# Hybrid decoder trunk on one core: loads and casts two chunks ahead, activation parts side by side, transposes behind products

## The chip, the cores and the metric

The kernel runs on one core of a Trainium2 chip. The metric is device time in microseconds of one launch, the median of several runs. The engines are named as in the profile: PE is TensorE (PEld its weight loads), DVE is VectorE, ACT is ScalarE, POOL is GpSimd, SP is the SyncE queue that issues all DMAs here.

## What is computed

Two layers over 256 tokens of 1024 channels, in float32. Cut to what matters here:

```python
hn = rms_norm(x, norm1_g)
proj = hn @ w_in                      # 1024 x 8216, 15 pieces
o_gla = gla_mixer(g_q, g_k, g_v, log_sigmoid(g_a @ up + b) / 16)     # decay per channel
mq, mk = (apply_rope(rms_norm(heads(a), g)) for a in (m_q, m_k))
y_moba = moba_mixer(mq, mk, m_v)      # softmax attention, 8 heads of 64
h_ml = mlstm_mixer(conv(l_q), conv(l_k), l_v, log_i, log_f)
gates = sigmoid(br_gate + gate_b)     # three branches of 1024
mixed = gates[0] * (y_gla @ w_gla) + gates[1] * (y_moba @ w_moba) + gates[2] * (y_mlstm @ w_mlstm)
x = x + mixed @ w_out
x = x + square(relu(rms_norm(x, norm2_g) @ w_ff1)) @ w_ff2
```

## The kernel before, in words

**Chunks.** All large weights lie in memory as chunks of 128 x 2048 floats (1 MB), 74 per layer, and the list ORDER (lines 152 to 155) fixes in which order they are used, both layers in a row. `prepare` (158) loads a chunk into one of three raw buffers with a DMA on SP and calls `split` (143): ACT rounds the chunk to the fast fp32r type as `hi`, DVE computes the rest `lo = raw - hi`, both in two halves of 128 x 1024, into one of three buffers each. `chunk` (171) hands out a chunk and first prepares all up to AHEAD (26) chunks behind it. The activations are kept in the same two parts: class `Norm` (189) writes `h` on ACT and `l` on DVE, channels on partitions. Each product of two numbers is then three matmuls: hi x h, lo x h, hi x l.

**Kinds of products.** `tok` (288) takes two chunks (a = 0, 1) and makes 256 tokens x 512 channels: per chunk 24 matmuls of 512 columns into two PSUM banks, one per token half. `chan_pair` (241) takes one chunk and makes 256 channels x 256 tokens, weights stationary: 48 matmuls of 256 columns into one bank. It makes gq, gk, lq (664 to 678) and the 16 chunks of `ff1` (775) of each layer. PSUM has eight banks: four in the pool pmm for these products, four in pmx for transposes and small products.

**A layer.** First the small weights ("s"), then mk (chunks 10, 11), the first gate (20, 21), mq (8, 9), the second gate (22, 23), mv, gv, gq, gk, and so on. `rope` (346) evicts mk or mq scaled by the norm factor (`scaled`, 301), squares and sums it, and rotates it with tables; of the two token halves DVE takes one and POOL the other (358). The decays of the GLA branch are the small products z (397 to 406), then logarithms, running sums and the exponentials eb and en (435 to 452; en is multiplied on POOL). The three mixers moba, gla and mlstm are generators, advanced a step at a time between the projections (646 to 725), the rest of mlstm behind the last gate. Then for each half of the channels three branch products br (728 to 740), each multiplied by its gate on DVE, the sum taken on DVE or, for the second branch, on POOL; then the transposes mt of the result (743 to 750), the output projection wo (753 to 769), the second norm, and the feed-forward part: ff1 of one chunk alternating with ff2 of another (775 to 827).

**What sets the order.** The framework's scheduler puts each engine's instructions into one fixed order at build time, by a priority that follows the program text and by when its cost model expects the operands. `tc.high_priority()` moves a block up; `after(i, j)` (60) puts instruction i behind j on their engine without a wait. DMAs keep the order of issue on SP, and an issue waits there until its buffer is free.

The initial loads are in lines 99 to 105, `late_loads` (129) follows the first mk chunk. The head of the layer loop reads:

```python
sh, sl_ = chunk(l, "s")
if l == 0:
    for k in range(4, 8):
        norm.parts(k, xTs[1][:, k - 4])
...
bmk = []
tok("mk", 10, 0, bmk)
```

Of the kernel before, what the change touches and what calls it, by code (L numbers as in the profile page):

```python
# [10 lines left out]
F32R = mybir.dt.float32r  # L11
# [3 lines left out]
OP = mybir.AluOpType  # L15
# [10 lines left out]
AHEAD = 1  # L26
# [17 lines left out]
def kernel(ctx: ExitStack, tc: tile.TileContext, xT, xtok, gbias, wbig, wsml, aup, cst, prm, out):  # L44
# [48 lines left out]
    nc.scalar.preload_act_table_set("exp_and_others")  # L93
# [6 lines left out]
    nc.sync.dma_start(xTs[0][:, 0:2], xT[:, 0:2, :])  # L100
    nc.sync.dma_start(raws[0][:, :512], wsml[0][:, :512])
    nc.sync.dma_start(xTs[0][:, 2:4], xT[:, 2:4, :])
    nc.sync.dma_start(raws[0][:, 512:], wsml[0][:, 512:])
    for p in range(2):
        nc.sync.dma_start(xTs[1][:, 2 * p:2 * p + 2], xT[:, 4 + 2 * p:6 + 2 * p, :])

    ident = cs[:, C_ID:C_ID + P]
# [21 lines left out]
    def late_loads():  # L129
# [13 lines left out]
    def split(tag, raw, n):  # L143
        hi = wspl.tile([P, CHW], F32R, tag="hi", name=f"hi{tag}")
        lo = wspl.tile([P, CHW], F32R, tag="lo", name=f"lo{tag}")
        for c in range(0, n, n // 2):
            sl = slice(c, c + n // 2)
            nc.scalar.copy(hi[:, sl], raw[:, sl])  # L148
            nc.vector.tensor_sub(lo[:, sl], raw[:, sl], hi[:, sl])  # L149
        return hi, lo  # L150
# [90 lines left out]
    def chan_pair(name, w, rh, rl, ks=range(KT), bank=None):  # L241
# [33 lines left out]
    for k in range(4):  # L275
        norm.parts(k, xTs[0][:, k])

    for l in range(DEPTH):
# [22 lines left out]
        def scaled(name, bs):  # L301
            o = slab(name, shape=(P, 2, 512))
            for t in range(2):
                nc.scalar.activation(o[:, t], bs[t].t, AF.Copy, scale=r[:, t:t + 1])
            return o
# [3 lines left out]
        if l == 0:  # L309
            for k in range(4, 8):  # L310
                norm.parts(k, xTs[1][:, k - 4])
        sh, sl_ = (a[:, :D].rearrange("p (k c) -> p k c", c=P) for a in (sh, sl_))
        bsm = Bank(pmm, f"sm{l}", [P, 512])
# [7 lines left out]
        if l == 0:  # L321
            late_loads()
            for t in range(2):
                for n in range(2):
                    norm.squares(t, n)
# [16 lines left out]
        if l + 1 < DEPTH:  # L342
            nc.sync.dma_start(raws[l + 1], wsml[l + 1])


        def rope(w, nm, bs):
            u = scaled(nm + "u", bs)
# [9 lines left out]
            for t in range(2):  # L357
                eng = nc.vector if t == 0 else nc.gpsimd
# [3 lines left out]
                eng.tensor_mul(r3, u[:, t].rearrange("p (h d) -> p h d", d=64), c3)  # L362
# [31 lines left out]
        rok, rsk = rope(1, "mk", bmk)  # L394
# [3 lines left out]
        for p in range(2):  # L398
            b = Bank(pmx, f"z{l}{p}", [P, 2, T])
            for n in range(2):  # L400
                h = 2 * p + n
                b.mm(b.t[:, n], us[:, h * P:(h + 1) * P], gs, True, True)
            for n in range(2):
                h = 2 * p + n
                nc.vector.tensor_scalar(mz[:, h], b.t[:, n], ab[:, h:h + 1], 0.0, op0=OP.add, op1=OP.min)
                nc.scalar.activation(az[:, h], b.t[:, n], AF.Abs, bias=ab[:, h:h + 1])
# [9 lines left out]

        gates = []

        def gate(i):
            bias = half(f"gb{l}{i}")  # L420
            nc.sync.dma_start(bias, gbias[l, i])
            bs = []
            tok(f"bg{i}", 20 + 2 * i, 0, bs)
            tok(f"bg{i}", 20 + 2 * i, 1, bs)
            g = slab(f"gate{i}", shape=(P, 2, 512))
            gates.append(g)
            for t in range(2):
                nc.vector.scalar_tensor_tensor(g[:, t], bs[t].t, r[:, t:t + 1], bias, op0=OP.mult, op1=OP.add)  # L428
                nc.scalar.activation(g[:, t], g[:, t], AF.Tanh, scale=0.5)

        gate(0)
# [231 lines left out]
        for p in range(2):  # L663
            b = chan_pair(f"gq{l}{p}", chunk(l, 4 + p), xh, xl)
            nc.vector.tensor_mul(qd[:, 2 * p:2 * p + 2], b.t, eb[:, 2 * p:2 * p + 2])
            step(M)
        for p in range(2):
            b = chan_pair(f"gk{l}{p}", chunk(l, 6 + p), xh, xl)
            nc.vector.tensor_mul(ki[:, 2 * p:2 * p + 2], b.t, en[:, 2 * p:2 * p + 2])
            step(M)  # L670
# [6 lines left out]
        for p in range(2):  # L677
            b = chan_pair(f"lq{l}{p}", chunk(l, 14 + p), xh, xl)
            nc.vector.tensor_mul(lqk[:, 2 * p:2 * p + 2, 3:], b.t, rT2)
# [44 lines left out]
        for _ in range(12):  # L724
            step(L)
# [3 lines left out]
        for hf in range(2):  # L729
            for br, (yh_, yl_) in enumerate((yg, (ymh, yml), yl)):  # L730
                w = [a.rearrange("p (k c) -> p k c", c=512) for a in chunk(l, 32 + 2 * br + hf)]
                g = gates[2 * br + hf]
                for t in range(2):
                    ts = slice(t * P, (t + 1) * P)
                    b = Bank(pmm, f"br{l}{br}{hf}{t}", [P, 512])
                    for k in range(4):
                        rows_mm(b, w, k, slice(0, 512), yh_[:, k, ts], yl_[:, k, ts], k == 0, k == 3)
                    nc.vector.scalar_tensor_tensor(g[:, t], g[:, t], 1.0, b.t, op0=OP.add, op1=OP.mult)  # L738
                    if br:
                        (nc.gpsimd if br == 1 else nc.vector).tensor_add(g[:, t], g[:, t], gates[2 * br - 2 + hf][:, t])  # L740
# [10 lines left out]


        norm = Norm(f"b{l}", q[:, Q_G2:Q_G2 + 8])
        ob = [[Bank(pmm, f"wo{l}{t}{n}", [P, 512]) for n in range(2)] for t in range(2)]
        for a in range(2):
            for n in range(2):
                w = [z.rearrange("p (k c) -> p k c", c=512) for z in chunk(l, 38 + 2 * a + n)]
                for t in range(2):
                    ts = slice(t * P, (t + 1) * P)
                    b = ob[t][n]  # L760
# [14 lines left out]
        def ff1(p):  # L775
            b = chan_pair(f"f1{l}_{p}_", chunk(l, 42 + p), norm.h, norm.l)
# [3 lines left out]
            s = half(f"fs{p}", shape=(P, 2, T))  # L780
            nc.vector.tensor_scalar(s, b.t, 0.0, None, op0=OP.max)
            nc.scalar.activation(s, s, AF.Square)  # L782
# [161 lines left out]
```

## Time and profile before

| | us |
|---|---|
| median of 3 runs (lowest, highest) | 935.83 (934.37, 935.89) |
| profiled execution, whole time | 934.08 |
| profiled execution, span from first to last instruction | 932.3 |

The profile is of one execution. Busy times of PE are modelled at their ends, so a busy PE isn't PE at its peak; the start-to-start distance of products tells its rate. Time that an engine waits is put down to what came last. All sums are made against the profiled execution.

### The profile page before, as it was taken

The page shows a single profiled execution, that of the slowest core. Times are in us where ns is not written, and L with a number is a line of the kernel's source. Part 1 is how long each engine was busy: PE and PEld are TensorE (multiplying, and loading weights), DVE is VectorE, ACT ScalarE, POOL GpSimd, SP SyncE. Part 2 cuts the span into 40 slices and gives each one's busy share as a digit, 9 for nine tenths or more (in the row PEclk, how much of TensorE's full clock was granted, in tenths as well). Part 3 has the DMA queues.
Part 4 walks back from the last instruction along what each step waited for, and adds up shares of the span by engine and source line. Part 5 has one row for each costly group of instructions (what it writes and reads, how often), then busy time and mean ns, then how long its engine had stood idle before and what let it go on. Part 6 is the DMA issues. An engine that isn't in the chain of part 4 may idle for free.

```text
span 932.3 us, 12890 instructions
## 1 busy us (share of the span) xinstructions
PE 905.4 (97%) x5188; PEld 793.9 (85%) x5188; DVE 628.6 (67%) x992; ACT 454.0 (49%) x647; POOL 73.3 (8%) x90
## 2 busy tenths in 40 slices
PE   7799999999999999999999999999999999999998
PEld 5578999888789999999887789988877799999996
DVE  5996668568867655555669966766788675555553
ACT  5765544455336444444557564445543554444441
POOL 2552000000210000000002300000013000000000
PEclk9799999999999999999999999999999999999999
DMA  8646443545444555555543564344545555555541
GB/s 325 217 164 246 177 147 110 218 151 188 162 160 175 187 188 199 194 180 183 181 169 114 192 226 151 131 161 167 192 147 180 181 182 181 181 187 192 196 148 45
DMA packets 26203, 164.92 MB, mean 177 GB/s; under 512 B 3040, under 2 KB 3296, under 8 KB 7328
## 3 DMA queue, kind: packets, MB, share of 16 engines
q1 hardware_dynamic: 26144, 164.11, 49.6%
q8 instruction: 40, 0.66, 0.3%
q14 instruction: 19, 0.16, 0.1%
HBM read 163.05 MB, written 1.05 MB: 176 GB/s over the span
## 4 chain that ended last, share of the span: by engine, by line
PE 85%; DVE 11%; issue 1%; ACT 1%; DMA 1%; SPq 0%; POOL 0%; DVEq 0%; ACTq 0%
PE fa L75 19%; PE bg L75 10%; PE wo L75 5%; DVE lo L149 4%; PE br L75 3%; PE gk L75 2%; PE lq L75 2%; PE gq L75 2%; PE lv L75 2%; PE lo L75 2%; PE mv L75 2%; PE gv L75 2%; PE gg L75 2%; PE mk L75 2%; PE sc L75 1%
## 5 line engine op out<-in xcount | busy, mean ns | idle before, releaser
L148 ACT CAST hi<-raw 128x1024 fp32r<-128x1024 f32 x296 | 301.4, 1048 | 368.0 <-issue 97.8
L149 DVE TENSOR_TENSOR lo<-raw,hi 128x1024 fp32r<-128x1024 f32 x296 | 363.3, 1247 | 142.5 <-ACT hi L148 142.1
L75 PE MATMUL fa<-hi,fh 128*128 128x512 f32 x512 | 162.4, 390 | 0.0
L75 PEld LDWEIGHTS fa<-hi,fh 128*128 128x128 f32 x512 | 96.3, 188 | 19.6
L75 PE MATMUL fa<-lo,fh 128*128 128x512 f32 x256 | 100.0, 391 | 0.0
L75 PE MATMUL bg<-lo,xha 128*128 128x512 f32 x192 | 76.2, 397 | 4.8 <-DVE lo L149 4.8
L75 PE MATMUL bg<-hi,xha 128*128 128x512 f32 x192 | 76.8, 401 | 4.1 <-ACT hi L148 4.1
L75 PE MATMUL bg<-hi,xla 128*128 128x512 f32 x192 | 75.8, 395 | 0.0
L75 PEld LDWEIGHTS fa<-lo,fh 128*128 128x128 f32 x256 | 48.2, 188 | 8.9
L75 PEld LDWEIGHTS bg<-lo,xha 128*128 128x128 f32 x192 | 36.8, 191 | 13.5 <-DVE lo L149 6.4
L75 PEld LDWEIGHTS bg<-hi,xha 128*128 128x128 f32 x192 | 36.6, 191 | 11.5 <-ACT hi L148 4.3
L75 PEld LDWEIGHTS bg<-hi,xla 128*128 128x128 f32 x192 | 36.7, 191 | 7.7
L75 PE MATMUL wo<-hi,mh 128*128 128x512 f32 x64 | 25.7, 401 | 0.0
L75 PE MATMUL wo<-hi,ml 128*128 128x512 f32 x64 | 25.0, 391 | 0.0
L75 PE MATMUL wo<-lo,mh 128*128 128x512 f32 x64 | 24.9, 389 | 0.0
L428 DVE SCALAR_TENSOR_TENSOR gate<-bg,ny,gb 128x512 f32<-128x512 f32 x24 | 17.3, 748 | 7.7 <-PE bg L75 7.7
L784 DVE TENSOR_TENSOR fh<-fs,fh 128x512 fp32r<-128x512 f32 x32 | 21.9, 684 | 0.0
L782 ACT ACTIVATE fs<-fs 128x512 f32<-128x512 f32 x32 | 20.1, 627 | 0.0
L738 DVE SCALAR_TENSOR_TENSOR gate<-gate,br 128x512 f32<-128x512 f32 x24 | 16.3, 680 | 5.3 <-PE br L75 5.3
L783 ACT CAST fh<-fs 128x512 fp32r<-128x512 f32 x32 | 19.7, 617 | 0.0
L475 ACT ACTIVATE pe<-pe,mn 128x128 f32<-128x128 f32 (+1 forms) x32 | 14.3, 449 | 10.1 <-DVE mn L473 10.1
L75 PE MATMUL lq<-xha,hi 128*128 128x256 f32 x64 | 18.8, 294 | 0.0
(550 smaller groups left out, 2218.3 us busy)
## 6 DMA issues: line engine op xcount, KB each, us to landing
raw<-in_wbig_dram SPq DMA_DIRECT2D x147, 1024.0 KB, 4.8
gb<-in_gbias_dram SPq DMA_DIRECT2D x12, 256.0 KB, 3.2
xT<-in_xT_dram SPq DMA_DIRECT2D x4, 256.0 KB, 4.9
raw<-in_wbig_dram SPq DMA_DIRECT2D x4, 256.0 KB, 6.2
x<-in_xtok_dram SPq DMA_DIRECT2D x2, 512.0 KB, 8.8
out_dram<-x SPq DMA_DIRECT2D x4, 256.0 KB, 2.1
cs<-in_cst_dram SPq DMA_DIRECT2D x1, 768.0 KB, 10.2
raws<-in_wsml_dram SPq DMA_DIRECT2D x2, 256.0 KB, 4.1
```

The source lines that it names most:

```text
L75: self._chain(nc.tensor.matmul(o, lhsT=lhsT, rhs=rhs, start=start, stop=stop, skip_group_check=True))
L148: nc.scalar.copy(hi[:, sl], raw[:, sl])
L149: nc.vector.tensor_sub(lo[:, sl], raw[:, sl], hi[:, sl])
L428: nc.vector.scalar_tensor_tensor(g[:, t], bs[t].t, r[:, t:t + 1], bias, op0=OP.mult, op1=OP.add)
L475: nc.scalar.activation(pe[:, cols], pe[:, cols], AF.Exp, bias=mn[:, i], scale=-1.0, accum_out=sums[:, i])
L738: nc.vector.scalar_tensor_tensor(g[:, t], g[:, t], 1.0, b.t, op0=OP.add, op1=OP.mult)
L782: nc.scalar.activation(s, s, AF.Square)
L783: nc.scalar.copy(h[:, 0], s)
L784: nc.vector.tensor_sub(h[:, 1], s, h[:, 0])
```

## The change

Two chunks are prepared ahead instead of one. The first loads are issued by one loop in the same order; the input x is loaded ahead of the constants, and with it the first raw chunks; the parameters and small weights of layer 1 are loaded behind the first gate. The parts of the first norm and the split of the small weights are one high-priority block. `h` and `l` become one tile `hl` with the two parts side by side per channel block, and `chan_pair` multiplies the hi weights with both at once (512 columns) into two banks, one per 128 channels; ACT copies the half from `l` and DVE adds the other. The weights of these chunks are laid out for it. `rope` does both token halves on DVE, and the evictions of mk stand behind the casts of chunk 21. The z products (`decays`) go between the two chunks of the first gate. eb, en and dec come after the rotation of mq, en on DVE. The gate's first DVE step gets high priority. The last steps of mlstm go between the branch products, the transposes mt behind a later branch product and behind the first chunk of wo, and the second branch's sum to DVE.

```diff
-AHEAD = 1
+AHEAD = 2
...
+    def load_x():
         for t in range(2):
             nc.sync.dma_start(x[:, t], xtok[:, t])
+
+    def load_constants():
         nc.sync.dma_start(cs, cst)
...
-        for l in range(1, DEPTH):
-            nc.sync.dma_start(prm_t[l], prm[l])
...
+        behind[tag] = i, j
         return hi, lo
...
-            self.h = act.tile([P, KT, T], F32R, tag="xh", name=f"xh{tag}")
-            self.l = act.tile([P, KT, T], F32R, tag="xl", name=f"xl{tag}")
+            self.hl = act.tile([P, KT, 2, T], F32R, tag="xhl", name=f"xhl{tag}")
+            self.h, self.l = self.hl[:, :, 0], self.hl[:, :, 1]
...
-        wh, wl = (a.rearrange("p (k c) -> p k c", c=T) for a in w)
-        b = bank or Bank(pmm, name, [P, 2, T])
-        for k in ks:
-            for n in range(2):
-                c = slice(n * P, (n + 1) * P)
-                b.mm(b.t[:, n], wh[:, k, c], rh[:, k], k == 0 and n == 0, False)
-                b.mm(b.t[:, n], wh[:, k, c], rl[:, k], False, False)
-                b.mm(b.t[:, n], wl[:, k, c], rh[:, k], False, k == KT - 1)
-        return b
+        wh, wl = (a.rearrange("p (n k c) -> p n k c", n=2, c=P) for a in w)
+        for n in range(2):
+            b = Bank(pmm, f"{name}{n}", [P, 2, T])
+            for k in range(KT):
+                b.mm(b.t, wh[:, n, k], hl[:, k], k == 0, False)
+                b.mm(b.t[:, 0], wl[:, n, k], hl[:, k, 0], False, k == KT - 1)
+            nc.scalar.copy(os[n], b.t[:, 1])
+            nc.vector.tensor_add(os[n], os[n], b.t[:, 0])
...
-    for k in range(4):
-        norm.parts(k, xTs[0][:, k])
+
+    def first_parts(c):
+        for k in (range(2, 6) if c == 0 else range(6, 8)):
+            norm.parts(k, xTs[k // 4][:, k % 4])
+
+    with tc.high_priority():
+        for k in range(2):
+            norm.parts(k, xTs[0][:, k])
+        ready[0, "s"] = split("s0", raws[0], D, first_parts)
+    done[0] = 1
...
-        bsm = Bank(pmm, f"sm{l}", [P, 512])
+        bsm = Bank(pmx if l == 0 else pmm, f"sm{l}", [P, 512])
...
-                eng = nc.vector if t == 0 else nc.gpsimd
+                eng = nc.vector
...
-        rok, rsk = rope(1, "mk", bmk)
+        rok, rsk = rope(1, "mk", bmk, behind[f"{l}_21"])
...
+            tok(f"bg{i}", 20 + 2 * i, 0, bs)
+            between()
+            tok(f"bg{i}", 20 + 2 * i, 1, bs)
...
+        gate(0, decays)
+        if l + 1 < DEPTH:
+            nc.sync.dma_start(prm_t[l + 1], prm[l + 1])
+            nc.sync.dma_start(raws[l + 1], wsml[l + 1])
...
-        nc.gpsimd.tensor_mul(en, en, rT4)
-
-        tok("mq", 8, 1, bmq)
-        roq, rsq = rope(0, "mq", bmq)
+        nc.vector.tensor_mul(en, en, rT4)
...
-            b = chan_pair(f"gq{l}{p}", chunk(l, 4 + p), xh, xl)
-            nc.vector.tensor_mul(qd[:, 2 * p:2 * p + 2], b.t, eb[:, 2 * p:2 * p + 2])
+            chan_pair(f"gq{l}{p}", chunk(l, 4 + p), norm.hl, [qd[:, 2 * p + n] for n in range(2)])
+            nc.vector.tensor_mul(qd[:, 2 * p:2 * p + 2], qd[:, 2 * p:2 * p + 2], eb[:, 2 * p:2 * p + 2])
...
-        for _ in range(12):
-            step(L)
+        step(L)
...
+                    if br:
+                        nc.vector.tensor_add(g[:, t], g[:, t], gates[2 * br - 2 + hf][:, t])
+                if hf == 0:
+                    step(L)
+                elif br == 0:
+                    merged(0)
...
+                if a == 0 and n == 0:
+                    merged(1)
...
-            nc.vector.tensor_scalar(s, b.t, 0.0, None, op0=OP.max)
-            nc.scalar.activation(s, s, AF.Square)
+            nc.vector.scalar_tensor_tensor(s, s, 0.0, s, op0=OP.max, op1=OP.mult)
```

## Rows read from the trace of the kernel before

**Rows 1.** The page: busy time of each engine, and the last chain's shares by engine.

```profile
PE 905.4 (97%) x5188; PEld 793.9 (85%) x5188; DVE 628.6 (67%) x992; ACT 454.0 (49%) x647; POOL 73.3 (8%) x90
...
PE 85%; DVE 11%; issue 1%; ACT 1%; DMA 1%; SPq 0%; POOL 0%; DVEq 0%; ACTq 0%
```

**Rows 2.** The chain that ended last, in order of time: start us, us, what.

```profile
93.66 5.75 PE gq L75 x48
...
309.86 5.47 PE fa L75 x24
```

**Rows 3.** Waits of PE: line, waited for, us in total, times, longest.

```profile
PE sm L75 <- ACT his L148: 6.2, 1, 6.2
PE bg L75 <- DVE lo L149: 4.8, 3, 2.7
PE bg L75 <- ACT hi L148: 4.1, 1, 4.1
PE mt L78 <- DVE gate L740: 2.6, 4, 0.9
PE z L75 <- DVE gs L393: 2.1, 1, 2.1
PE mv L75 <- DVE lo L149: 1.1, 1, 1.1
PE yl0b L78 <- DVE ymls L627: 0.8, 1, 0.8
```

**Rows 4.** Windows: length, busy (count) of PE, PEld, DVE, ACT, POOL; clock, DMA, GB/s.

```profile
30.00:40.00 10.00, 8.09 (x25) 6.62 (x26) 10.00 (x21) 4.93 (x8) 3.38 (x3) 0.61 0.37 128
23.40:66.60 43.20, 34.89 (x141) 27.71 (x138) 41.82 (x58) 31.11 (x41) 21.90 (x20) 0.88 0.52 188
130.00:164.00 34.00, 34.00 (x225) 30.99 (x224) 29.24 (x68) 14.00 (x28) 0.11 (x1) 1.00 0.33 118
310.00:460.00 150.00, 150.00 (x956) 136.85 (x955) 83.68 (x83) 68.55 (x83) 0.00 (x0) 1.00 0.53 188
480.00:530.00 50.00, 46.30 (x205) 37.45 (x204) 46.40 (x66) 32.09 (x42) 14.55 (x12) 1.00 0.45 159
```

**Rows 5.** Timeline of PE in 23 to 48 us: start us, us, instruction [idle before].

```profile
27.96 1.22 PE L75 MATMUL bg<-hi,xha 128*128 128x512 f32 x2 [4.09 <-ACT hi L148]
31.91 0.80 PE L75 MATMUL bg<-lo,xha 128*128 128x512 f32 x1 [2.73 <-DVE lo L149]
```

**Rows 6.** Timeline of ACT, then DVE, in 9 to 72 us.

```profile
8.56 1.71 ACT L199 ACTIVATE xha<-xT,prm 128x256 fp32r<-128x256 f32 x4 [0.73 <-DMA xT<-in_xT_dram]
...
23.00 0.69 ACT L304 ACTIVATE mku<-mk,ny 128x512 f32<-128x512 f32 x1 [3.77 <-PE mk L75]
...
26.86 2.94 ACT L148 CAST hi<-raw 128x1024 fp32r<-128x1024 f32 x3
...
29.56 3.43 DVE L149 TENSOR_TENSOR lo<-raw,hi 128x1024 fp32r<-128x1024 f32 x2
```

**Rows 7.** Groups of DVE and POOL by line: busy us, mean ns | idle before.

```profile
L362 DVE TENSOR_TENSOR mkro<-mku,tabs 128x512 f32<-128x512 f32 x2 | 1.4, 686 | 2.0 <-ACT mku L304 2.0
L362 DVE TENSOR_TENSOR mqro<-mqu,tabs 128x512 f32<-128x512 f32 x2 | 5.8, 2898 | 0.0
L149 DVE TENSOR_TENSOR lo<-raw,hi 128x1024 fp32r<-128x1024 f32 x296 | 363.3, 1247 | 142.5 <-ACT hi L148 142.1
L740 POOL TENSOR_TENSOR gate<-gate,gate 128x512 f32<-128x512 f32 x8 | 14.0, 1765 | 36.9 <-DVE gate L738 36.9
L452 POOL TENSOR_TENSOR az<-az,rTa 128x1024 f32<-128x1024 f32 x2 | 6.5, 3254 | 24.4 <-ACT az L450 24.4
```

**Rows 8.** Groups of ACT and DVE that read 128x256 from PSUM.

```profile
L237 ACT COPY rTa<-nb2a 128x256 f32<-128x256 f32 x2 | 0.7, 354 | 0.0
L390 DVE TENSOR_TENSOR sm<-sm,rTa 128x256 f32<-128x256 f32 x2 | 0.8, 414 | 0.0
```

More of the change, by code (lines that the diff above doesn't have):

```diff
@@ L99 @@
     nc.sync.dma_start(prm_t[0][:, :Q_RG], prm[0][:, :Q_RG])
[L100 to L105, printed above, removed]
+    for p in range(4):
+        nc.sync.dma_start(xTs[p // 2][:, 2 * (p % 2):2 * (p % 2) + 2], xT[:, 2 * p:2 * p + 2, :])
+        if p < 2:
+            nc.sync.dma_start(raws[0][:, 512 * p:512 * p + 512], wsml[0][:, 512 * p:512 * p + 512])
+    nc.scalar.preload_act_table_set("exp_and_others")
     ident = cs[:, C_ID:C_ID + P]
@@ L141, with split @@
     nc.gpsimd.tensor_copy(ms[64:], rows[64:])
-    def split(tag, raw, n):
+    behind, evacuated = {}, {}
+    def split(tag, raw, n, between=lambda c: None):
         hi = wspl.tile([P, CHW], F32R, tag="hi", name=f"hi{tag}")
@@ L147, in split @@
             sl = slice(c, c + n // 2)
-            nc.scalar.copy(hi[:, sl], raw[:, sl])
-            nc.vector.tensor_sub(lo[:, sl], raw[:, sl], hi[:, sl])
+            i = nc.scalar.copy(hi[:, sl], raw[:, sl])
+            j = nc.vector.tensor_sub(lo[:, sl], raw[:, sl], hi[:, sl])
+            between(c)
+        behind[tag] = i, j
         return hi, lo
@@ L299, in tok, with scaled @@
                     bs[t].mm(bs[t].t, xl[:, kk, ts], wh[:, k], False, kk == 7)
-        def scaled(name, bs):
+        def scaled(name, bs, first=None):
             o = slab(name, shape=(P, 2, 512))
-            for t in range(2):
-                nc.scalar.activation(o[:, t], bs[t].t, AF.Copy, scale=r[:, t:t + 1])
+            with tc.high_priority():
+                for t in range(2):
+                    i = nc.scalar.activation(o[:, t], bs[t].t, AF.Copy, scale=r[:, t:t + 1])
+                    if first:
+                        after(i, first)
+            evacuated[name] = i
             return o
@@ L309 @@
         if l == 0:
-            for k in range(4, 8):
-                norm.parts(k, xTs[1][:, k - 4])
+            load_x()
         sh, sl_ = (a[:, :D].rearrange("p (k c) -> p k c", c=P) for a in (sh, sl_))
-        bsm = Bank(pmm, f"sm{l}", [P, 512])
+        bsm = Bank(pmx if l == 0 else pmm, f"sm{l}", [P, 512])
         for k in range(KT):
@@ L335 @@
         nc.gpsimd.tensor_sub(us[64:96], up[64:96], us[64:96])
+        hr = small("hr", [P, 2])
+        nc.gpsimd.tensor_scalar(hr, r, 0.5, None, op0=OP.mult)
         tabs = act.tile([P, 4, 2, 64], F32, tag="tabs", name=f"tabs{l}")
@@ L341, with rope @@
         tok("mk", 10, 1, bmk)
[L342 to L347, printed above, removed]
+        def rope(w, nm, bs, first=(None, None)):
+            u = scaled(nm + "u", bs, first[0])
             ss = small(nm + "ss", [P, 16])
@@ L361, in rope @@
                 c3 = tabs[:, 2 * w, t][:, None, :].to_broadcast([P, 8, 64])
-                eng.tensor_mul(r3, u[:, t].rearrange("p (h d) -> p h d", d=64), c3)
+                i = eng.tensor_mul(r3, u[:, t].rearrange("p (h d) -> p h d", d=64), c3)
+                if first[1]:
+                    after(i, first[1])
                 tmp = half(f"{nm}tmp{t}")
@@ L393, with gate, decays @@
         nc.vector.tensor_sub(gs[32:64], sm[32:64], gs[32:64])
-        rok, rsk = rope(1, "mk", bmk)
-        mz, az = slab("mz"), slab("az")
[L398 to L406, printed above, removed]
+        rok, rsk = rope(1, "mk", bmk, behind[f"{l}_21"])
+        gates = []
+        def gate(i, between=lambda: None):
+            bias = half(f"gb{l}{i}")
+            nc.sync.dma_start(bias, gbias[l, i])
+            bs = []
+            tok(f"bg{i}", 20 + 2 * i, 0, bs)
+            between()
+            tok(f"bg{i}", 20 + 2 * i, 1, bs)
+            g = slab(f"gate{i}", shape=(P, 2, 512))
+            gates.append(g)
+            with tc.high_priority():
+                for t in range(2):
+                    nc.vector.scalar_tensor_tensor(g[:, t], bs[t].t, r[:, t:t + 1], bias, op0=OP.mult, op1=OP.add)
+            for t in range(2):
+                nc.scalar.activation(g[:, t], g[:, t], AF.Tanh, scale=0.5)
+        mz, az = slab("mz"), slab("az")
+        def decays():
+            for p in range(2):
+                b = Bank(pmx, f"z{l}{p}", [P, 2, T])
+                for n in range(2):
+                    h = 2 * p + n
+                    b.mm(b.t[:, n], us[:, h * P:(h + 1) * P], gs, True, True)
+                for n in range(2):
+                    h = 2 * p + n
+                    nc.vector.tensor_scalar(mz[:, h], b.t[:, n], ab[:, h:h + 1], 0.0, op0=OP.add, op1=OP.min)
+                    nc.scalar.activation(az[:, h], b.t[:, n], AF.Abs, bias=ab[:, h:h + 1])
+        gate(0, decays)
+        if l + 1 < DEPTH:
+            nc.sync.dma_start(prm_t[l + 1], prm[l + 1])
+            nc.sync.dma_start(raws[l + 1], wsml[l + 1])
         mf, af = quarter("mf"), quarter("af")
@@ L414 @@
         nc.scalar.activation(az, az, AF.Ln, bias=1.0)
[L417 to L431, printed above, removed]
         bmq, bmv, bgv, bgg, blv, blo = [], [], [], [], [], []
@@ L677 @@
         for p in range(2):
-            b = chan_pair(f"lq{l}{p}", chunk(l, 14 + p), xh, xl)
-            nc.vector.tensor_mul(lqk[:, 2 * p:2 * p + 2, 3:], b.t, rT2)
+            o = lqk[:, 2 * p:2 * p + 2, 3:]
+            chan_pair(f"lq{l}{p}", chunk(l, 14 + p), norm.hl, [o[:, n] for n in range(2)])
+            nc.vector.tensor_mul(o, o, rT2)
             for n in range(2 * p, 2 * p + 2):
@@ L723, with merged @@
         gate(5)
-        for _ in range(12):
-            step(L)
+        step(L)
         mh, ml = [], []
[L729 to L740, printed above, removed]
+        def merged(hf):
+            g = gates[4 + hf]
             mh.append(slab(f"mh{hf}", F32R))
@@ L750 @@
                 nc.vector.scalar_tensor_tensor(ml[hf][:, sl], b.t, 0.5, mh[hf][:, sl], op0=OP.mult, op1=OP.subtract)
+        for hf in range(2):
+            for br, yp in enumerate((yg, (ymh, yml), yl)):
+                w = [a.rearrange("p (k c) -> p k c", c=512) for a in chunk(l, 32 + 2 * br + hf)]
+                yh_, yl_ = yp
+                g = gates[2 * br + hf]
+                for t in range(2):
+                    ts = slice(t * P, (t + 1) * P)
+                    b = Bank(pmm, f"br{l}{br}{hf}{t}", [P, 512])
+                    for k in range(4):
+                        rows_mm(b, w, k, slice(0, 512), yh_[:, k, ts], yl_[:, k, ts], k == 0, k == 3)
+                    nc.vector.scalar_tensor_tensor(g[:, t], g[:, t], 1.0, b.t, op0=OP.add, op1=OP.mult)
+                    if br:
[4 more added lines that the diff above has]
+                    merged(0)
         norm = Norm(f"b{l}", q[:, Q_G2:Q_G2 + 8])
-        ob = [[Bank(pmm, f"wo{l}{t}{n}", [P, 512]) for n in range(2)] for t in range(2)]
+        ob = [[Bank(pmm, f"wo{l}{t}{n}", [P, 512]) for t in range(2)] for n in range(2)]
         for a in range(2):
@@ L775, in ff1 @@
         def ff1(p):
-            b = chan_pair(f"f1{l}_{p}_", chunk(l, 42 + p), norm.h, norm.l)
+            s = half(f"fs{p}", shape=(P, 2, T))
+            chan_pair(f"f1{l}_{p}_", chunk(l, 42 + p), norm.hl, [s[:, n] for n in range(2)])
             if p == 0:
@@ L860, in _chan @@
     n = w.shape[1] // T
-    return [w[:, T * j:T * (j + 1)].reshape(KT, P, T).transpose(1, 0, 2).reshape(P, CHW) for j in range(n)]
+    return [w[:, T * j:T * (j + 1)].reshape(KT, P, 2, P).transpose(1, 2, 0, 3).reshape(P, CHW) for j in range(n)]
 def _tok(w):
```

23 lines of the change are left out of this document (11 added, 12 removed).

## The prediction

> **What bounds the kernel now.** I read the page first: TensorE is busy 97% of the span, DVE 67%, ScalarE 49%, GpSimd 8%, and the chain that ended last is 85% PE [rows 1]. So the kernel is bound by the rate of products, and the next thing to find is where PE waits. The chain in order of time gives the rate in steady stretches: a chunk of 24 products of 512 columns takes 5.47 us (228 ns each), a channel pair of 48 products of 256 columns 5.75 us (120 ns each) [rows 2]. PE's own waits name the places [rows 3]: the first load, the casts of the gate chunks, the z products and mv of layer 1, and the transposes mt, yl0b and yl1b (the row of yl1b is like that of yl0b, two such rows in all).
>
> The windows weigh these waits by what they cost [rows 4]. In 23.4 to 66.6 us PE did 141 matmuls, at most 141 x 0.228 = 32.1 us of work, in 43.2 us: 11.1 us are lost. In 480 to 530 us, the same place of layer 1, 205 x 0.228 = 46.7 of 50: 3.3 us are lost. In 310 to 460 us nothing is lost; in the first stretch DVE is busy 41.82 of 43.2 us, in the second 46.40 of 50. The head of a layer is therefore bound by DVE's queue as much as by PE, and everything behind it by PE alone.
>
> **The change, part by part.**
>
> *Paired activation parts.* A channel pair (22 per layer: two gq, two gk, two lq, 16 ff1) now issues 16 products of 512 columns (the hi weight against h and l side by side) and 16 of 256, instead of 48 of 256. At the rates of [rows 2] that is 16 x 0.228 + 16 x 0.120 = 5.56 us against 5.75: 0.187 us less, x 44 = **8.2 us**. The ends: no gain, if a 512-column product between narrow ones costs as much as two narrow ones; no loss, since the columns stay 12,288 and the instructions fall by a third. I take the upper end, because both shapes stand in steady streams in [rows 2]. The Trainium skill has a rule that speaks against this term (TensorE: Matmul & The Clock Gate, section Back-to-back issue gap): columns over 2.4 GHz plus 2.5 ns. It gives 109 and 216 ns, a pair of 5.24 us against 5.20, and 44 x 0.04 = 1.8 us in all; the rows, 11 to 12 ns above it for both shapes, decide here.
>
> The price of pairing is eviction. Each pair now takes two banks, and each bank one ScalarE copy (0.354 us for 128x256) and one DVE add (0.414 us) [rows 8]. The multiply behind them keeps its size (in ff1 one DVE operation of 128x512 replaces another, and ScalarE's square goes). So DVE gains 0.83 us a pair. In the feed-forward window a pair lasts some 11.2 us, so 150 us hold 13.4 pairs and 11 us more of DVE work beside 83.68: hidden. In 130 to 164 us DVE is at 29.24 of 34, and two lq pairs add 1.7 us into 4.8 us of free time: tight. Banks come round every second pair, 11 us or more in ff1 and 5.6 us in gq and gk. For queueing behind these adds I charge **2 us** over both layers; ends 0 and 6.
>
> *Loads and casts two chunks ahead, layer 0.* Now ScalarE waits 3.77 us for the products of mk, evicts them, and only at 26.86 casts chunk 20; DVE's two halves follow at 29.56, taking 3.43 us [rows 6]. PE waits 4.09 us for the first and 2.73 us for the second [rows 5], and then runs at a granted clock of 0.61 in 30 to 40 us [rows 4]. There 25 matmuls took 8.1 us after the wait ended, against 25 x 0.228 = 5.7: some 2.4 us more. These three make 9.2 of the 11.1 us. With AHEAD = 2 the raw load of chunk 20 passes the constants and parameters on SP's queue, its cast stands before the eviction of mk, and the eviction is tied behind the cast of chunk 21. ScalarE's idle 3.77 us hold the two halves of chunk 20 at 1.05 each (an estimate from 2.94 for three). The constants land later by one 1 MB load; rope's tables can bear that, since the DVE multiplies are now put behind the cast of chunk 21. On SP the second layer's parameters move behind the first gate's bias: they are wanted in layer 1 only, so this costs nothing. What is held back are mk's evictions, by up to two casts (2 us), and with them the two banks that mq wants; in front of mq PE has 48 gate products, 10.9 us. Elsewhere looking further ahead moves little: the three buffers for hi and lo stay, so a cast still waits for the products of three chunks before.
>
> DVE's work sets how much of this lasts. Rope's second half and the multiply of en come over from GpSimd. Per layer that is, for mk, 0.69 + 2 x 0.41 + 0.69 + 0.69 = 2.9; for mq 2.2; for en, at the price of a 128x1024 operation, 1.25 [rows 7, 8]: 6.3 us more. In return the overlap goes: the same L362 multiply costs 0.686 us alone and 2.898 beside GpSimd's 3.254 us multiply of en, and the two casts at 29.56 took 3.43 instead of 2 x 1.247 = 2.5 [rows 6, 7]. These two rows return 3.1 us; with the smaller operations around them I take 6.3 as returned, so DVE's work stays level and only begins earlier. Since a full DVE gives some time back later, I take **7.5 us** of the 9.2; ends 2 and 11.1.
>
> *Decays between the gate's two halves, layer 1.* z waits 2.1 us for gs and mv 1.1 us for a cast [rows 3]. The z products now have 5.5 us of gate products in front, and casts come earlier: **2.7 us** of the 3.3; ends 0 and 3.3.
>
> *Transposes moved.* The mt transposes (2.6 us of waits in four) go behind a branch chunk or a chunk of wo, 5.5 us of products that need nothing from them; GpSimd's add, 1.765 us [rows 7], becomes a DVE add on the way. yl0b and yl1b wait 0.8 us each; they now stand behind a branch chunk, but an order made from readiness already put products there, so I count half. Together 2.6 + 0.8 = **3.4 us**; ends 0 and 4.2. What is late next: the casts of the following branch chunks on DVE, with two more adds among them.
>
> *Start.* The second half of the small weights' cast comes after two parts whose data let ScalarE start at 8.56 only [rows 6]: **0.4 us** more; ends 0 and 1.5 (two parts at 1.71 / 4 and one short cast). The load order there is unchanged.
>
> Sum: -8.2 + 2 - 7.5 - 2.7 - 3.4 + 0.4 = -19.4. The profiled execution took 934.08 us (span 932.3), so 914.7. It lies 1.75 below the median of the three runs and 0.3 below the lowest; allowing a little for that, **915**.
>
> **Rivals.**
>
> *The waits only move (0.20).* PE comes earlier and meets DVE's queue: casts of chunks 8 and 9 behind rope. For it: DVE full in [rows 4]. Against: with that same load PE's waits for lo at a gate, past the first 2.73, are only 2.1 us in both layers [rows 3, 5]. Layer 0 gives 2, layer 1 nothing: 934.1 - 8.2 - 2 - 3.4 + 2.4 = 923.
>
> *Pairing pays little (0.07).* The 512-column product brings no saving because the columns, not the instruction, set the rate. Against it stand the two rates of [rows 2]. 914.7 + 8.2 = 923. By the Trainium skill's rule (TensorE: Matmul & The Clock Gate, Back-to-back issue gap) the time would be 914.7 + 8.2 - 1.8 = 921.
>
> *Slower: DVE becomes the bound of both heads and of lq (0.10).* The place is DVE's queue between a layer's mk and its lv. Rope on both halves stands ahead of the casts of 8 and 9, and if the overlap with GpSimd returns nothing, each layer's head grows by the 6.3 us moved. Six pairs a layer add 5 us more where DVE is 86% busy, half of it on the path. 934.1 - 8.2 - 3.4 + 12.6 + 5 = 940. It decides once PE's waits for lo, 4.8 + 1.1 = 5.9 us now [rows 3], exceed some 17.5 us, the 11.6 of pairing and transposes on top.
>
> That the edits land without effect, the scheduler keeping its order, is covered for the transposes by the end 0.
>
> **How the numbers follow.** Forecast 0.60; waits move 0.20; pairing pays little 0.07; slower 0.10; and 0.03 for a mixture that ends at no change. A measurement of this kernel can tell 0.2%, 1.9 us, from none. Faster 0.87, same 0.03, slower 0.10. The range: at the low end the heads give 14.4 instead of 10.2, nothing queues (2), the transposes give 0.8 more and the start loses nothing (0.4); 914.7 less these 7.4 is 907, and 1 us of spread between runs makes 906. The high end must hold both 923 cases and 4 us more of queueing: 927.
>
> **What would show it.** Right: gq, gk, lq and ff1 stretches of 32 products in about 5.56 us; no wait on a cast between mk and the first gate, and a granted clock near 1.0 in 30 to 40 us; L362 at 0.69 for mq; no wait in front of mt; matmuls fewer by 44 x 16 = 704. Wrong: PE's waits for lo in 35 to 75 us above some 6 us; waits of pair products for a DVE add or a ScalarE copy; PE's first product of mk much after 12 us.

## The result and the profile after

The changed kernel takes 922.71 us (median of 4 runs, 921.5 to 923.6) against 935.1 of the kernel before on the same chip: ratio 0.9868, 95% interval 0.985 to 0.9885, or 12.4 us less. The sign and the range (906 to 927) held; the forecast of 915 missed by 7.7 us, and the time is that of the rival "the waits only move", 923. The page of the changed kernel, as [rows 1]:

```profile
PE 902.0 (98%) x4484; PEld 757.5 (82%) x4484; DVE 650.8 (71%) x1108; ACT 470.3 (51%) x705; POOL 40.5 (4%) x62
...
PE 90%; DVE 6%; ACT 1%; DMA 1%; issue 1%; SPq 0%; DVEq 0%
```

There are 704 matmuls fewer, as the prediction said, and DVE has 22 us more to do. The chain that ended last, in two stretches (start us, us, what), answers to [rows 2]:

```profile
99.72 5.55 PE gq L75 x32
...
305.19 5.45 PE fa L75 x24
310.64 5.64 PE f L75 x32
```

A channel pair is 32 products now. In the feed-forward part it takes 5.64 us, not the 5.56 forecast; the chunk of ff2 (fa), whose products kept their shape, takes what it took. PE's waits (line, waited for, us in total, times, longest), as [rows 3]:

```profile
PE sm L75 <- ACT his L148: 5.9, 1, 5.9
PE gv L75 <- DVE gate L423: 5.5, 2, 3.6
PE mq L75 <- DVE lo L149: 1.6, 2, 1.2
PE mqT L78 <- DVE mqro L381: 1.1, 2, 0.9
PE mv L75 <- DVE lo L149: 0.7, 1, 0.7
PE mk L75 <- DVE lo L149: 0.5, 1, 0.5
PE sc L75 <- ACT qz L396: 0.3, 1, 0.3
```

All the waits that the change aimed at are gone: both casts at bg, z, mt, yl0b and yl1b. In their place stand new ones: 1.6 us for casts at mq, and the rest between the start of mv and the start of gq: gv, mqT, mv, sc. A windows view shows both halves of this (length, busy time and count of PE, PEld, DVE, ACT, POOL; clock, DMA, GB/s). The first two rows answer to the first two of [rows 4], the last two run from mv's first product to gq's first, in layer 0 and in layer 1:

```profile
30.00:40.00 10.00, 8.78 (x41) 6.99 (x40) 10.00 (x23) 6.64 (x9) 0.95 (x1) 1.00 0.62 228
23.40:56.60 33.20, 31.57 (x142) 25.37 (x141) 31.43 (x52) 23.85 (x33) 8.76 (x16) 1.00 0.69 265
60.83:92.83 32.00, 27.78 (x114) 21.75 (x113) 22.78 (x37) 15.13 (x21) 11.50 (x10) 0.89 0.47 170
515.07:544.87 29.80, 26.13 (x117) 21.48 (x116) 20.95 (x29) 14.28 (x19) 6.61 (x2) 0.94 0.57 200
```

The same stretch of work, mv's first product to gq's first, in the kernel before:

```profile
69.29:93.31 24.02, 24.02 (x118) 20.12 (x116) 16.56 (x22) 13.28 (x18) 6.39 (x7) 1.00 0.69 251
524.35:549.78 25.43, 24.34 (x118) 20.04 (x116) 18.79 (x28) 13.28 (x18) 1.49 (x3) 1.00 0.66 237
```

From 23.4 us on, as many matmuls as filled 43.2 us (141, here 142) fit into 33.2, at a granted clock of 1.00. Then mv and gv, which took 24.02 us before, take 32.00, and in layer 1 29.80 instead of 25.43. Cutting both traces at the first starts of PE's products gives the whole balance:

| stretch, us | before | after | difference |
|---|---|---|---|
| start to mv, layer 0 | 69.29 | 60.83 | -8.46 |
| mv to gq, layer 0 | 24.02 | 32.00 | +7.98 |
| gq to br, layer 0 | 137.50 | 135.83 | -1.67 |
| br to wo, layer 0 | 37.09 | 35.05 | -2.04 |
| wo to layer 1 | 205.08 | 203.15 | -1.93 |
| layer 1 to its mv | 51.37 | 48.21 | -3.16 |
| mv to gq, layer 1 | 25.43 | 29.80 | +4.37 |
| gq to br, layer 1 | 137.50 | 135.82 | -1.68 |
| br to wo, layer 1 | 37.09 | 35.05 | -2.04 |
| wo to the last product | 203.73 | 201.85 | -1.88 |

The heads gain 11.6 us up to mv and return 12.4 right behind it. What is left of the gain, 7.2 us in the four stretches from gq to br and from wo on, which hold the channel pairs, and 4.1 from br to wo, which holds the transposes, is nearly the whole of these 10.5 us (the executions profiled lie 1.0 below and 0.9 above the medians of this comparison, hence 10.5 here and 12.4 there).

What DVE does ahead of mv is in its timeline, in 52 to 70 us (start us, us, instruction):

```profile
52.37 0.69 DVE L373 TENSOR_TENSOR mqro<-mqu,tabs 128x512 f32<-128x512 f32 x1
...
54.98 1.23 DVE L460 TENSOR_TENSOR mz<-mz,az 128x1024 f32<-128x1024 f32 x1
...
56.72 2.43 DVE L463 TENSOR_TENSOR_SCAN az<-cs,mz 128x256 f32<-128x256 f32 x4
...
59.64 1.22 DVE L467 TENSOR_TENSOR mz<-az 128x1024 f32<-128x1024 f32 x1
...
63.28 1.22 DVE L476 SCALAR_TENSOR_TENSOR eb<-eb,rTa 128x1024 f32<-128x1024 f32 x1
64.41 1.41 DVE L423 SCALAR_TENSOR_TENSOR gate<-bg,ny,gb 128x512 f32<-128x512 f32 x2
...
66.66 1.21 DVE L477 TENSOR_TENSOR az<-az,rTa 128x1024 f32<-128x1024 f32 x1
...
68.02 1.21 DVE L149 TENSOR_TENSOR lo<-raw,hi 128x1024 fp32r<-128x1024 f32 x1
```

From 52.37 to 68.02, 15.65 us, DVE makes no cast: it does the rotation of mq, the running sums and exponentials of the decays, and the gate's eviction. In the kernel before, the sums and eb stood among the casts of chunks 9, 22 and 23, and en was on GpSimd; counted from the first chunk on, the first lo of chunk 12 came there at:

```profile
67.55 1.21 DVE L149 TENSOR_TENSOR lo<-raw,hi 128x1024 fp32r<-128x1024 f32 x1
```

That is 0.47 us earlier than 68.02. The change brings PE to mv 8.46 us earlier, but not DVE to the cast that mv needs. ScalarE's timeline shows when the hi parts of that time were ready, mv's first two halves by about 57 us (the first two of these four):

```profile
55.05 3.89 ACT L148 CAST hi<-raw 128x1024 fp32r<-128x1024 f32 x4
```

So it is DVE's queue that holds lo back, not its input. PE reaches mv at 60.83, and its timeline shows what it meets:

```profile
60.83 0.62 PE L75 MATMUL mv<-hi,xhla 128*128 128x512 f32 x2
61.29 0.71 PE L78 MATMUL mkT<-cs,mkro 128*128 128x128 f32 x5
62.91 0.44 PE L78 MATMUL mqT<-cs,mqro 128*128 128x128 f32 x2 [0.92 <-DVE mqro L381]
65.31 1.06 PE L75 MATMUL gv<-hi,xhla 128*128 128x512 f32 x2 [1.96 <-DVE gate L423]
...
69.29 0.79 PE L75 MATMUL mv<-lo,xhla 128*128 128x512 f32 x1 [0.72 <-DVE lo L149]
69.88 0.63 PE L75 MATMUL mv<-hi,xhla 128*128 128x512 f32 x1
70.31 0.63 PE L75 MATMUL mv<-lo,xhla 128*128 128x512 f32 x1
```

It can do two products of mv and five transposes of mk; then transposes of mq and two products of gv wait for DVE (the wait at gv is for the gate's eviction, which stands in the same queue). mv goes on at 69.29, and its products first start 0.43 us apart, from 74.4 us on 0.23 apart. A windows view of the two stretches gives the granted clock, 0.50 and 1.00:

```profile
69.29:74.15 4.86, 4.86 (x12) 3.80 (x12) 4.86 (x7) 0.00 (x0) 3.52 (x2) 0.50 0.50 162
74.42:80.00 5.58, 5.58 (x26) 4.60 (x25) 4.06 (x5) 2.01 (x2) 1.83 (x2) 1.00 0.95 399
```

The first is the lower of the clock's two levels, 1.2 GHz; in the 8.3 us before it PE was busy for 4.1.

### The profile page after: what moved, and what is told of

Its sections match the earlier page's. It is cut to its first block, busy times and chain, and to the rows that moved or that the text cites. A ratio compares the mean times of both kernels' runs of the same rounds, so it can differ in the third digit from the quotient of the medians.

```text
span 921.8 us, 11634 instructions
## 1 busy us (share of the span) xinstructions
PE 902.0 (98%) x4484; PEld 757.5 (82%) x4484; DVE 650.8 (71%) x1108; ACT 470.3 (51%) x705; POOL 40.5 (4%) x62
## 3 DMA queue, kind: packets, MB, share of 16 engines
HBM read 163.05 MB, written 1.05 MB: 178 GB/s over the span
## 4 chain that ended last, share of the span: by engine, by line
PE 90%; DVE 6%; ACT 1%; DMA 1%; issue 1%; SPq 0%; DVEq 0%
PE f L75 20%; PE fa L75 19%; PE bg L75 11%; PE br L75 7%; PE wo L75 5%; PE mv L75 3%; PE gk L75 2%; PE gq L75 2%; PE lq L75 2%; PE lv L75 2%; PE lo L75 2%; PE gg L75 2%; PE mk L75 2%; PE gv L75 2%; DVE lo L149 2%; PE pv L75 1%
## 5 line engine op out<-in xcount | busy, mean ns | idle before, releaser
L75 PE MATMUL f<-xhlb,hi 128*128 128x512 f32 x512 | 181.4, 398 | 0.0
L75 PE MATMUL f<-xhlb,lo 128*128 128x256 f32 x512 | 142.8, 280 | 0.0
L75 PE MATMUL bg<-hi,xhla 128*128 128x512 f32 x384 | 122.3, 392 | 0.0
L75 PEld LDWEIGHTS f<-xhlb,hi 128*128 128x128 f32 x512 | 96.0, 188 | 22.9
L75 PEld LDWEIGHTS f<-xhlb,lo 128*128 128x128 f32 x512 | 96.6, 189 | 1.2
L75 PEld LDWEIGHTS bg<-hi,xhla 128*128 128x128 f32 x384 | 72.0, 188 | 14.6
L75 PE MATMUL bg<-lo,xhla 128*128 128x512 f32 x192 | 74.8, 389 | 0.0
L75 PEld LDWEIGHTS bg<-lo,xhla 128*128 128x128 f32 x192 | 36.1, 188 | 7.0
L252 ACT COPY fs<-f 128x256 f32<-128x256 f32 x64 | 23.7, 370 | 24.9 <-PE f L75 24.7
L253 DVE TENSOR_TENSOR fs<-fs,f 128x256 f32<-128x256 f32 x64 | 26.6, 416 | 3.1 <-ACT fs L252 3.1
```

The lines of the kernel that those rows point to most:

```text
L75: self._chain(nc.tensor.matmul(o, lhsT=lhsT, rhs=rhs, start=start, stop=stop, skip_group_check=True))
L252: nc.scalar.copy(os[n], b.t[:, 1])
L253: nc.vector.tensor_add(os[n], os[n], b.t[:, 0])
```

## The experiments

The theory: PE gains what the change meant it to gain, arrives at mv 8 to 9 us earlier, and meets work in DVE's queue that was there before as well, but had been worked off by the time PE came. The rivals: PE's own order of products, the GpSimd work moved to DVE, and too little gain from pairing.

**The sums and exponentials behind mv.** In the changed kernel, mf, rows, the scans, bx, dec, eb and en go behind mv's second chunk in the program text, and nothing else moves there. The scheduler lays out each engine's order anew from that text: PE now does the whole first chunk of mv ahead of the transposes.

```diff
-        nc.vector.tensor_sub(mf[R4], mf[R4], af[R4])
...
-        nc.vector.tensor_mul(en, en, rT4)
...
+        nc.vector.tensor_sub(mf[R4], mf[R4], af[R4])
...
+        nc.vector.tensor_mul(en, en, rT4)
...
         tok("gv", 0, 0, bgv)
```

> The kernel after, with the running sums and exponentials of the decays (from the mf subtraction to dec) written behind mv's second chunk instead of around mq's. First theory, DVE's queue: in the kernel after, DVE does 15.6 us of work without a cast (52.4 to 68.0 us) while the hi half of chunk 12 has been ready since 57 us, so mv stands until its lo comes at 69.3. With the sums and exponentials (9 us of DVE work) out of the way the first lo of chunk 12 comes some 4 to 6 us earlier, mv's products start before 64 us, the half-rate stretch behind them goes, and gq starts at 85 to 88 us instead of 92.8; layer 1 gives 2 to 4 us. 913 to 917 us in all, ratio 0.977 to 0.981. Rival, PE's order: the transposes of mq and the first products of gv, which stand in front of mv's lo products, wait for their own operands (mqro, the gate's eviction) and keep the stall where it is: 920 to 923, ratio 0.984 to 0.987. Second rival, DVE's total: the work only moves and its queue is as long by the time of gq: 920 to 923 too, but with the wait moved to gq or the attention's first scores.

Measured: 908.77 us, ratio 0.9718 (0.9703 to 0.9732), 14 us below the changed kernel, 4 us below the range that the theory gave, and faster than both kernels. PE's waits, all there are:

```profile
PE sm L75 <- ACT his L148: 5.8, 1, 5.8
PE mq L75 <- DVE lo L149: 1.6, 2, 1.2
PE mk L75 <- ACT hi L148: 0.7, 1, 0.7
PE mk L75 <- DVE lo L149: 0.5, 1, 0.5
```

Windows from mv's first product to gq's first, both layers:

```profile
59.59:83.33 23.74, 23.74 (x115) 19.79 (x113) 22.79 (x30) 16.68 (x22) 6.29 (x9) 1.00 0.59 222
505.66:529.70 24.04, 24.04 (x117) 20.11 (x116) 21.65 (x29) 16.56 (x22) 1.54 (x2) 1.00 0.62 225
```

PE is busy throughout, DVE nearly so: the block now runs while PE has products at hand. DVE's timeline shows the two stages that changed places:

```profile
57.58 1.22 DVE L149 TENSOR_TENSOR lo<-raw,hi 128x1024 fp32r<-128x1024 f32 x1
...
60.96 1.21 DVE L149 TENSOR_TENSOR lo<-raw,hi 128x1024 fp32r<-128x1024 f32 x1
...
68.09 1.85 DVE L667 TENSOR_TENSOR_SCAN az<-cs,mz 128x256 f32<-128x256 f32 x3
```

The first lo of mv's chunk is cast at 57.58 instead of 68.02, the scans come at 68.09 instead of 56.72. The 8.3 and 5.8 us that the two stretches shrink by are 14.0 us, as much as the medians differ by (the two profiled executions differ by 15.1; the other 1.2 lie ahead of mv, with mk starting 1.3 earlier). This fits the theory, and gives more than it asked, above all in layer 1 (5.8 us instead of 2 to 4). That PE's order changed along with DVE's is taken up in the next run. Which of the block's parts (scans, or eb and en) costs most was not separated.

**PE's order.** In the changed kernel the transposes mkT are held behind the first chunk of mv, mqT behind the first of gv.

```diff
-        def head_rows(nm, ro):
+        def head_rows(nm, ro, bs):
...
+                b.last = bs[1].last
```

> The kernel after, with the transposes of mk tied behind the first chunk of mv, and those of mq behind the first chunk of gv, on PE. DVE's queue theory: PE finds no lo of chunk 12 either way, so it stands in front of mv instead of in front of mqT, until about 69 us in layer 0; the transposes, 2 us of work that lay in the stall, come on top: 922 to 925, ratio 0.986 to 0.989. The PE order rival: the stall was made by the transposes that were pulled ahead, and goes: 914 to 917, ratio 0.978 to 0.981.

Measured: 926.75 us, ratio 0.9911 (0.9896 to 0.9927), 4 us worse than the changed kernel. The waits between mv and gq got longer:

```profile
PE gv L75 <- DVE gate L424: 8.3, 2, 4.4
...
PE mv L75 <- DVE lo L149: 3.3, 2, 2.8
```

The time lies 1.8 us above the theory's range, and far from the rival's 914 to 917. With fewer other things to do, PE only waits more for the same DVE results. Two products of gv still stand ahead of mv's lo products in this run, and hold nothing back: DVE casts the first lo of chunk 12 at 67.23 to 68.44 us, and PE takes it at 68.50 (DVE's row, then PE's):

```profile
67.23 1.21 DVE L149 TENSOR_TENSOR lo<-raw,hi 128x1024 fp32r<-128x1024 f32 x1
```

```profile
68.50 0.80 PE L75 MATMUL mv<-lo,xhla 128*128 128x512 f32 x1 [2.83 <-DVE lo L149]
```

So the order of PE is not the cause; the place of the cast in DVE's queue is.

**GpSimd's half back.** In the changed kernel the second token half of rope and the multiply of en go back to GpSimd (and only DVE's half stays tied behind the casts of chunk 21).

```diff
-                eng = nc.vector
+                eng = nc.vector if t == 0 else nc.gpsimd
...
-        nc.vector.tensor_mul(en, en, rT4)
+        nc.gpsimd.tensor_mul(en, en, rT4)
```

> The kernel after, with rope's second token half and the multiply of en back on GpSimd, as in the kernel before. Per layer 6.3 us of DVE work go back. First theory (the overlap with GpSimd costs DVE what it saves): DVE's two-input operations beside GpSimd's slow down as before (an L373 multiply of mq near 2.9 us instead of 0.69), and the time stays: 921 to 925, ratio 0.985 to 0.989. Rival (the moved work is what fills DVE's queue in 52 to 68 us, and the overlap is cheap): 915 to 919, ratio 0.979 to 0.983. Third, the move was worth more than the work: above 926, ratio over 0.990.

Measured: 926.38 us, ratio 0.9906 (0.9891 to 0.9921), 3.7 us worse, the third expectation. PE's waits for lo at mv are now 11.1 us:

```profile
PE mv L75 <- DVE lo L149: 11.1, 3, 5.5
```

So taking this work off DVE does not end its lateness. Layer 0 reaches gq about as early as in the changed kernel (92.03 against 92.83 us); the loss lies in layer 1, where mv to gq takes 32.34 us instead of 29.80, and the stretch ahead of it 1.0 more. DVE's and then GpSimd's timeline, in 60 to 64 us, show what sharing costs:

```profile
60.86 2.33 DVE L184 TENSOR_SCALAR mqy<-mqss 128x16 int32<-128x16 int32 x1
```

```profile
60.50 2.66 POOL L477 TENSOR_TENSOR az<-az,rTa 128x1024 f32<-128x1024 f32 x1 [7.52 <-ACT az L475]
```

An operation on 128x16 numbers takes 2.33 us and ends when GpSimd's multiply does (63.19 and 63.16 us); in the changed kernel the same one takes 0.17. The Trainium skill (SBUF — State Buffer, section Who interferes with whom) has the ports that the two engines share as an exclusive lock; the two rows agree.

**The same in the version with the late sums.**

> The version with the sums and exponentials behind mv, with rope's second half and the multiply of en back on GpSimd. With the block out of the way of the casts, what DVE and GpSimd do beside each other meets less of PE's wait: theory 909 to 912, a loss smaller than the 3.7 us that the same edit cost in the changed kernel. If the slow operations beside GpSimd still stand ahead of the casts of chunk 12: 912 or more.

Measured: 916.47 us, ratio 0.9802 (0.9789 to 0.9816): 7.7 us worse than 908.77. The expectation that the loss would be smaller there fell; the other one, 912 or more, held. PE waits 3.7 us for lo at mv of layer 1, 1.4 at the second gate of layer 0. That PE, with nothing else to wait for in the head, feels each microsecond of DVE more would fit this; it was not tested apart.

**Pairing alone, on the kernel before,** with its layout, its two banks and its evictions:

> The kernel before with the paired channel products alone (their layout, two banks, the new evictions; nothing else). With the mixed pair of products at 353 ns, as the trace of the kernel after has it, 44 pairs give 5 to 6 us: 930, ratio 0.993 to 0.995. By the two single rates of the kernel before (348 ns) it would be 8.2 us: 927.7, ratio 0.991. Rival: the second bank and the adds on a DVE that is full beside a slower GpSimd cost the heads and the lq stretch what the products save: 933 to 938, ratio 0.997 to 1.002.

Measured: 928.65 us, ratio 0.9923 (0.9902 to 0.9943), 7.2 us less. **Pairing taken out of the changed kernel** (one bank of 48 products of 256 columns, and the old evictions):

> The kernel after, with channel pairs as before: 48 products of 256 columns into one bank, the old evictions, the old layout of these weights (the tile with h and l side by side stays). The step of the prediction says 0.187 us for each of 44 pairs, 8.2 us: 931, ratio 0.995 to 0.997. The trace of the kernel after says less: gq, gk and lq pairs take 5.55 us (0.20 less than before, 12 pairs), but ff1 pairs 5.64 (0.11 less, 32 pairs), 2.4 + 3.6 = 6.0 us: 928.7, ratio 0.993. A third possibility, that the second bank and the extra evictions cost elsewhere in the projections what the products save: 922 to 926.

Measured: 928.65 us as well, ratio 0.9927 (0.9909 to 0.9945), 5.5 us more than the changed kernel's 0.9868; this is the 928.7 that the lengths of the pairs in the trace gave. So pairing is worth 5.5 to 7.2 us (some 2 us to either side), and the rival "pairing pays little" falls. By the formula in the Trainium skill (TensorE: Matmul & The Clock Gate, Back-to-back issue gap), which that page calls the gap of an isolated product, it would be worth an estimated 1.8 us; the measurement decides against that here.

**The moved steps alone, on the kernel before:** mlstm's last steps between the branch products, mt behind a later branch and behind wo's first chunk, the second branch's sum on DVE, the new bank order of wo.

> The kernel before with the end of a layer's mixers alone changed: mlstm's last steps between the branch products, the transposes mt behind a later branch chunk and behind wo's first chunk, the second branch's sum on DVE, wo's banks in the other order. The prediction's term is 3.4 us, both layers: 932.5, ratio 0.996 to 0.997. The stretch from the first br to the first wo in the kernel after is 2.0 us shorter per layer, so 4 us: 931.9, ratio 0.995 to 0.996. Rival: without pairing and casts two ahead the casts of the branch chunks on DVE become late, and little is left: ratio 0.998 to 1.000.

Measured: 930.07 us, ratio 0.9938 (0.9918 to 0.9958), 5.8 us less, more than expected. In its trace br to wo takes 35.04 and 35.06 us, as in the changed kernel: 2.04 less per layer, 4.1 in all. Another 0.4 us per layer come from gq to br (137.09 and 137.06 us instead of 137.50), where mlstm's last steps stood: 4.9 in all. The rest lies within the interval (1.9 us to either side).

**The heads alone:** the changed kernel without pairing and without the moved steps.

> The changed kernel with the old channel pairs and the old order from the last gate to wo: only the edits to the heads of the layers are left (two chunks ahead, the first gate's decays, rope and en on DVE, the start). Theory (DVE's queue ahead of the casts of chunk 12 gives the head's gain back): no change from the kernel before within 0.2%, 933 to 936. If the head kept what the prediction gave it, 10.2 us: 925. If the shortfall lay in the pairing alone, below 927.

Measured: 934.59 us, ratio 0.9989 (0.998 to 0.9998): 1 us, within 0.2% of no change. Its waits at gv are those of the changed kernel, while mt's are back:

```profile
PE gv L75 <- DVE gate L423: 5.5, 2, 3.6
PE mt L78 <- DVE gate L765: 3.1, 4, 1.2
```

This shows where the missing part of the forecast is: of 10.2 us for the heads, 1 came. The parts alone, 1, 5.5 to 7.2 for pairing and 5.8 for the moved steps, make 12.3 to 14.0, and the whole change 12.4.

**One chunk ahead instead of two,** in the changed kernel, then in the version with the late sums:

```diff
-AHEAD = 2
+AHEAD = 1
...
-        rok, rsk = rope(1, "mk", bmk, behind[f"{l}_21"])
+        rok, rsk = rope(1, "mk", bmk, behind[f"{l}_20"])
```

> The kernel after with one chunk prepared ahead (mk's evictions then stand behind the casts of chunk 20, since those of 21 come later). Theory, DVE's queue: the lead that PE gains at the first gate (9 to 10 us by the first mq product) comes from the early cast of chunk 20; with one ahead part of it goes, but what is lost there was given back at mv anyway, so the time stays within 3 us: 921 to 926, ratio 0.985 to 0.990. Rival, casts two ahead carry the whole of the head and the branch stretch: 928 to 934, ratio 0.992 to 0.999.

> The version with the sums and exponentials behind mv, now with one chunk ahead instead of two, the evictions of mk held behind the casts of the one chunk that is left. If the casts two ahead are what brings PE early to mq, and the moved block only keeps that, the gain of the moved block is mostly lost: 916 to 922. If the moved block alone does it, as good as with two ahead: 908 to 911.

Measured: 924.52 us (ratio 0.9884, 0.986 to 0.9907), hardly more than the changed kernel and in the theory's range; and 913.68 us (0.9772, 0.9759 to 0.9785), 4.9 more than 908.77. By the starts of gq, both lose in layer 0 (3.4 and 5.1 us). In layer 1 the first gains 3.0 us back, and the second stays as it is (a difference under 0.1). So casting two ahead pays in layer 0 of both; in the changed kernel layer 1 loses most of it again, and why was not followed up. Neither figure expected of the second came: 9 of the moved block's 14 us stay without the second chunk ahead.

**The late sums in the kernel before:**

> The kernel before with the sums and exponentials of the decays written behind mv's second chunk, as in the run that did it to the kernel after. Theory, DVE's queue is only met by a PE that comes early: PE's waits for lo in front of the second gate's last products and of mv are 1.7, 0.6 and 1.3 us in both layers, so at most 3.5 us come back: 932 to 936, ratio 0.996 to 1.000. Rival: the place of these sums costs the kernel before as much as the kernel after (14 us there), whatever PE does: 920 to 926, ratio 0.983 to 0.990.

Measured: 931.68 us, ratio 0.9957 (0.9942 to 0.9972), at the edge of what the theory allowed. The same move that is worth 14 us in the changed kernel is worth 4 here. So the place of these sums costs far more when PE comes early.

## Why the prediction was right in sign and 7.7 us off

*Paired parts: right, by two errors that nearly cancel.* Forecast 8.2 less 2 for queueing, net 6.2; measured 5.5 to 7.2 in the two runs. Per pair the table has 1.93 / 16 = 0.12 us in ff1. In the projections (gq to br) it has 1.67 us a layer, but 0.41 of these came with the moved steps alone; the run with pairing alone has 1.25 there, 1.25 / 6 = 0.21 a pair. Against 0.187 for all, that is 6.3 to 6.4 us in both layers; no wait of a pair's product for an eviction appears among PE's waits. So the gross term was too large in ff1, and the charge for queueing was not due.

*Transposes: right.* Forecast 3.4, ends 0 and 4.2; measured 4.1 from br to wo, and 0.8 more ahead of it, which the prediction did not count. mt, yl0b and yl1b wait no more, and no wait of PE shows DVE's added sums.

*Heads: this is the step that failed.* "Since a full DVE gives some time back later, I take 7.5 us of the 9.2", and 2.7 for layer 1. Up to mv both hold within a microsecond: 8.46 and 3.16 (counted from the first product of mk, layer 0 gains 9.6). The waits went and the clock rose from 0.61 to 1.00 in 30 to 40 us, as forecast. What failed is the word "some". In the heads, the prediction asked what is late next only for the casts of chunks 8 and 9, behind mk's rope, and found little; there PE waits 1.6 us. It did not follow DVE's queue one stage further, to mq's rotation, the decays' sums and exponentials and the gate's eviction, which together stand for 15.65 us ahead of the lo of chunk 12. DVE comes to that lo at 68.02 us, and at 67.55 before the change. In the kernel before PE came to mv at 69.29 us, and that covered them; at 60.83 nothing does. The giveback is 8.0 and 4.4 us. In layer 1 one wait of 3.6 for the gate makes most of it. In layer 0 the waits make some 4 us, and 12 products from 69.29 to 74.42 us at the lower clock another 5.1 - 12 x 0.228 = 2.4. The prediction's sign of being wrong, waits for lo above some 6 us in 35 to 75 us, did not show: they are 2.3, because PE meets other results of the same queue first, the gate and mqro, and waits 3.1 us for those.

*The rival "the waits only move" gave the right time by the right kind of mechanism, at the wrong place.* It named chunks 8 and 9, and kept 2 us of layer 0; at those casts only 1.6 us are lost, the place is mv, and the heads kept about 1 us in both layers. Its 923 is in part luck: it counts 8.2 us for pairing and 3.4 for the transposes, where some 6.4 and 4.9 came.

*The slower rival had the right engine and the wrong reason.* DVE did become what PE waits for, but the GpSimd work moved to it pays (3.7 us here, 7.7 in the faster version), since the overlap returned more than the move cost: mq's first multiply takes 0.69 us on DVE, as the prediction said, instead of 2.90 [rows 7].

*Start: not shown.* The term of 0.4 us is smaller than what one profile differs from the next by. mk starts 1.18 us later in the changed kernel's profile, but at 11.57 us in the version with the late sums, whose start is the same, against 11.66 before; in the runs that keep the old start it lies between 11.58 and 12.41.

*A reading that was off.* Three casts in 2.94 us are 0.98 us each, not 1.05; no term hangs on it.

## What to carry to other kernels

A wait that is removed moves the engine's arrival at everything behind it: take the time saved, go on along the other engine's queue in program order by that much, and look at what had been covered until then. Where an in-order engine serves both a stream of casts that the bottleneck needs now and a chain that is needed later, the place of the chain in that queue is worth as much as the waits themselves: here 14 us, more than the whole change. A part that shows no gain alone (the heads, 1 us) may need a second edit to show it.

## What the runs showed of the hardware that was not expected

In ff1, products of 512 and 256 columns that alternate cost a little more than in streams of their own: a channel pair takes 5.64 us for 16 of each, 353 ns for one of each, against 228 + 120 = 348 by [rows 2]. In gq it takes 5.55 us, 347 ns, so the alternation alone does not cost it; what does in ff1 stays open.

A tiny DVE operation can cost as much as a large one beside GpSimd: 2.33 us instead of 0.17 for 128x16 numbers, until a GpSimd multiply of 2.66 us ended. Here taking such multiplies off GpSimd paid, 3.7 and 7.7 us, though DVE is the busier engine.
